# Value products and modulation chunks issued in a row, the chunks spread between the steps of the q projection, five weight pieces loaded ahead

## The chip, the cores and the metric

The kernel runs on one core of a Trainium2 chip. Its time is the device time of one execution in microseconds. The matrix engine is called PE here (PEld is its weight load, which overlaps with it), the vector engine DVE, the scalar engine ACT, the general-purpose engine POOL, and the engine that issues most of the loads SP.

## What is computed

One inference step of a two-layer trunk on 512 latent tokens and 128 context tokens of width 1024, in 32-bit floats. Layer 0 is gated attention with 16 query heads and 4 key-value heads of width 64; layer 1 is a gated linear recurrence. In both layers the input is first modulated:

```python
mod = jax.nn.silu(cond) @ w + b            # shift, scale and gate, 3 x 1024, for two conditions
h   = x * (1.0 + scale) + shift
q, k, v, g = split(h @ w_in)               # attention: q 1024, k 256, v 256, g 1024 columns
q, k = rms_norm(q) , rms_norm(k)           # and axial rotary positions on the latent tokens
s = einsum('qd,sd->qs', q, keys) / 8       # 128 cached keys and 512 own ones for latent tokens
o = einsum('qs,sd->qd', softmax(s), vals)
out = (o * silu(g)) @ w_out
x = layer_norm(alpha * x + gate * out)
```

The modulation of layer 1 (shift, scale, gate) and the gate of layer 0 are not needed in the attention; they are computed beside it.

## The kernel before, in words

The work runs in five stages: a lead-in (modulation of layer 0, keys and values), the gates' and the first q projection, the attention, the output projection of layer 0 with its normalisation, and layer 1 with its own output projection. A tile scheduler takes the program's operations in their written order, reorders them by priority and by its own estimate of what is ready, and writes one in-order queue for each engine. Within a queue an instruction that waits holds up all behind it.

**Attention.** The work is cut into 36 units: for each of the 4 key-value heads c one unit for the context tokens and 8 for the latent ones (a query head and a half of the tokens). A unit has two `front` steps (scores into a PSUM tile `sc`, row maximum `nm` on DVE, exponential into `p` on ACT, later a division on POOL), and three transposing steps `trans`, each of which transposes blocks of `p` on PE into a PSUM tile `pt` and copies them to SBUF tiles `pts`: two copies of 128x512 on ACT and a last one of 128x256 on DVE (L728). When two units of a pair are done, `apply` multiplies the values by both of them: five key blocks k, each with two products of 64 output rows (`av_mms`, L750). The product of j=0 fills PSUM partitions 0 to 63 and that of j=1 partitions 64 to 127, so the two use different columns of the PE array. A unit's time is spent on all four engines, and the units are interleaved by `att_gen`.

**Side work.** While the attention runs, `weave` gives a list of side jobs a fraction `SIDE_B` of a step for each step of the attention. In order they are: the projection of the next head's q (`q_gen`: two weight pieces, 15 token tiles of 24 products over the three heads that are made here, a chain of RMS norm and rotation over ACT, DVE and POOL, and a transposition `qps`), then some modulation chunks (`ada_gen`), and so on for three heads; after them the last modulation chunks, which wait until the attention has reached its last head, then the first pieces of the output weights and a split of the gated output. When a head's first unit is due and its q is not finished, `side.until` runs the side work without pause until it is.

**A modulation chunk** needs two weight pieces of 512 KB. `ada_part` (L262) multiplies one piece with the conditions: four products, each into 32 of the 128 output partitions, so that they use four different column groups of the array. Two such parts are summed in PSUM; then come a copy to SBUF (L276), four small products with a selector (L285) and an addition. There are 16 chunks, handed out to four places by `ADA_CUT`.

**Loads.** `pump` issues the pieces in a fixed order on SP while fewer than `RAW_AHEAD` wait to be used. The pieces lie in the pool `rawp`.

## Time and profile before

| | us |
|---|---|
| three runs, median | 894.47 |
| three runs, lowest and highest | 894.38, 896.09 |
| the profiled execution | 891.1 |
| its span, first to last instruction | 889.3 |
| PE busy in it | 844.8 |
| attention stage, about 135 to 370 us: PE busy | 225.56 of 235.00 |
| layer 1 until its last head, 450 to 790 us: PE busy | 339.67 of 340.00 |
| last stretch, 790 to 889.3 us: PE busy | 81.62 of 99.30 |

The profile is a trace of one execution. In a row of the timeline stand the start in us, the duration in us, the engine, the line of the kernel, the operation, what it writes and reads, and how many instructions were merged; a product of two 32-bit tiles (L750, L262, L285, L305) shows as two PE instructions. A value in brackets is the idle time ahead of the row and what ended it. The end of a PE instruction is modelled and overlaps the next one's start, so the time that a piece of work takes on PE is read from start to start.

### The profile page before, as it was taken

The numbers are of one execution on the slowest core, as the hardware profiler recorded it, in microseconds if no ns is written. First come the engines' busy times: TensorE is split into PE (matmuls) and PEld (weight loads), VectorE is DVE, ScalarE is ACT, GpSimd is POOL, SyncE is SP. The second block draws the span as 40 slices with busy tenths as digits, with TensorE's granted clock in tenths as the row PEclk, the third lists the DMA queues.
The fourth block names the chain that finished last, engine by engine and source line by source line (L and its number), as shares of the span: only waits on it lengthen the run. The fifth ranks groups of instructions, "written<-read, shape, count | busy, mean of one in ns | idle before, by whom it ended". The sixth has DMA issues, their size and how long they took to land.

```text
span 889.3 us, 19146 instructions
## 1 busy us (share of the span) xinstructions
PE 844.8 (95%) x8076; PEld 736.4 (83%) x8076; DVE 539.0 (61%) x960; ACT 371.2 (42%) x732; POOL 212.6 (24%) x247
## 2 busy tenths in 40 slices
PE   6898999989999899999999999999999999988995
PEld 3588999858858656778899999999999999986774
DVE  3466335646655644676446677576768585758495
ACT  2232437545554745522244454444444444443200
POOL 0032003323323724510000133233333224110110
PEclk9999999999999999999999999999999999998998
DMA  9831210042051066271131313232332313232121
GB/s 359 328 107 54 81 39 25 2 164 75 1 194 45 3 218 208 90 242 48 57 117 51 102 56 117 63 98 77 91 95 79 101 55 107 64 111 99 54 95 71
DMA packets 30182, 89.84 MB, mean 101 GB/s; under 512 B 4401, under 2 KB 9009, under 8 KB 29073
## 3 DMA queue, kind: packets, MB, share of 16 engines
q1 hardware_dynamic: 19728, 72.03, 24.1%
q0 software_dynamic: 3168, 9.31, 3.7%
q10 hardware_dynamic: 7200, 7.29, 2.6%
q8 instruction: 63, 1.03, 0.5%
q14 instruction: 23, 0.18, 0.1%
HBM read 79.44 MB, written 9.18 MB: 100 GB/s over the span
## 4 chain that ended last, share of the span: by engine, by line
PE 76%; DMA 8%; DVE 7%; POOL 3%; ACT 3%; issue 2%; ACTq 0%; DVEq 0%; POOLq 0%
PE rps L1106 7%; PE rps L1107 6%; PE rps L1108 6%; PE vgps L1096 5%; PE pot L750 4%; PE vgps L1098 4%; PE vgps L1097 4%; PE pt L832 4%; DMA raw<-in_ada_w 3%; PE outp L984 3%; PE outp L985 3%; PE outp L986 3%; PE lv L1236 2%; PE adaps L262 2%; PE sc L723 2%
## 5 line engine op out<-in xcount | busy, mean ns | idle before, releaser
L1106 PE MATMUL rps<-h1hi,rhi 128*128 128x320 f32 x368 | 118.2, 321 | 0.0
L1107 PE MATMUL rps<-h1lo,rhi 128*128 128x320 f32 x368 | 113.7, 309 | 0.0
L1108 PE MATMUL rps<-h1hi,rlo 128*128 128x320 f32 x368 | 113.3, 308 | 0.0
L825 POOL TENSOR_SCALAR p<-p,rc 128x640 f32<-128x640 f32 x64 | 52.1, 816 | 104.1 <-DVE rc L824 101.2
L1106 PEld LDWEIGHTS rps<-h1hi,rhi 128*128 128x128 f32 x368 | 69.1, 188 | 1.3
L1107 PEld LDWEIGHTS rps<-h1lo,rhi 128*128 128x128 f32 x368 | 69.3, 188 | 0.0
L1108 PEld LDWEIGHTS rps<-h1hi,rlo 128*128 128x128 f32 x368 | 69.1, 188 | 0.0
L820 ACT ACTIVATE p<-sc,nm 128x640 f32<-128x640 f32 x64 | 51.1, 798 | 41.3 <-DVE nm L817 33.4
L817 DVE TENSOR_REDUCE nm<-sc 128x1 f32<-128x640 f32 x64 | 52.4, 820 | 24.3 <-PE sc L724 23.6
L222 DVE TENSOR_TENSOR rlo<-raw,rhi 128x1024 fp32r<-128x1024 f32 x32 | 46.1, 1441 | 33.9 <-ACT rhi L221 33.9
L1264 POOL COPY At<-near 32x160 f32<-32x160 f32 x32 | 14.0, 437 | 196.6 <-DVE near L1226 195.6
L1214 ACT COPY kc<-A 128x640 f32<-128x640 f32 x40 | 32.2, 805 | 59.0 <-DVE A L1245 51.6
L221 ACT CAST rhi<-raw 128x1024 fp32r<-128x1024 f32 x32 | 33.6, 1049 | 51.6 <-PE rps L1107 47.4
L832 PE MATMUL pt<-ident,p 128*128 128x128 f32 x320 | 51.2, 279 | 1.4 <-DVE pts L728 0.8
L1096 PE MATMUL vgps<-rhi,h1hi 128*128 128x256 f32 x180 | 51.4, 286 | 1.2 <-ACT h1hi L938 1.2
L1098 PE MATMUL vgps<-rhi,h1lo 128*128 128x256 f32 x180 | 50.5, 280 | 0.4 <-DVE h1lo L939 0.4
L1097 PE MATMUL vgps<-rlo,h1hi 128*128 128x256 f32 x180 | 50.5, 280 | 0.0
L750 PE MATMUL pot<-pts,vv 128*64 128x256 f32 x320 | 50.0, 390 | 0.0
L832 PEld LDWEIGHTS pt<-ident,p 128*128 128x128 f32 x320 | 36.8, 142 | 12.9 <-issue 6.7
L728 ACT COPY pts<-pt 128x512 f32<-128x512 f32 x64 | 36.0, 588 | 23.5 <-PE pt L832 23.2
L723 PE MATMUL sc<-kk,X 128*128 128x320 f32 x128 | 43.2, 345 | 0.4 <-ACT p L820 0.4
L332 PE MATMUL gps<-hhi,whi 128*128 128x320 f32 x128 | 40.8, 319 | 2.4 <-ACT X L582 2.4
(257 smaller groups left out, 2399.2 us busy)
## 6 DMA issues: line engine op xcount, KB each, us to landing
raw<-in_rec_w_in SPq DMA_DIRECT2D x40, 512.0 KB, 3.8
raw<-in_ada_w SPq DMA_DIRECT2D x32, 512.0 KB, 4.4
raw<-in_ada_w SPq DMA_DIRECT2D x8, 1024.0 KB, 11.3
raw<-in_attn_w_in SPq DMA_DIRECT2D x16, 512.0 KB, 4.2
raw<-in_attn_w_out SPq DMA_DIRECT2D x8, 512.0 KB, 4.4
raw<-in_rec_w_out SPq DMA_DIRECT2D x8, 512.0 KB, 4.1
h<-in_xT SPq DMA_DIRECT2D x8, 320.0 KB, 10.8
x1d<-y SPq DMA_DIRECT2D x5, 512.0 KB, 2.6
```

What stands on the lines that cost most here:

```text
L723: nc.tensor.matmul(out, X[:, h, t0:t0 + P], kk[:, c, k0:k1], start=True, stop=False)
L750: nc.tensor.matmul(pot[j * HD:(j + 1) * HD, :CW], vv[:, slot, c * HD:(c + 1) * HD], moving[j], start=first, stop=last)
L817: nc.vector.tensor_reduce(nm[:, 0:1], sc[:, :, :320], AX.XY, ALU.max, negate=True)
L820: nc.scalar.activation(halves(p[:]), sc[:, :, :320], AF.Exp, bias=nm[:, 0:1], accum_out=su[:, 0:1])
L825: nc.gpsimd.tensor_scalar(p, p, rs[:, 0:1], 1.0, ALU.mult, ALU.mult)
L832: nc.tensor.transpose(pt[:, i * 256 + q * P:i * 256 + (q + 1) * P], ps[q][:, (k0 + i) * P:(k0 + i + 1) * P], ident)
L1096: nc.tensor.matmul(out, h1hi[:, k, t], hi, start=(k == 0), stop=False)
L1097: nc.tensor.matmul(out, h1hi[:, k, t], lo, start=False, stop=False)
L1098: nc.tensor.matmul(out, h1lo[:, k, t], hi, start=False, stop=(k == KT - 1))
L1106: nc.tensor.matmul(ps[:, j, :320], hi[:, k, :], h1hi[:, k, t], start=(k == 0), stop=False)
L1107: nc.tensor.matmul(ps[:, j, :320], hi[:, k, :], h1lo[:, k, t], start=False, stop=False)
L1108: nc.tensor.matmul(ps[:, j, :320], lo[:, k, :], h1hi[:, k, t], start=False, stop=(k == KT - 1))
```

## The change

The lines of the changed kernel lie 1 to 13 lines further down: L262 becomes L263, L285 becomes L286, L580 becomes L582, L723 and L724 become L725 and L726, L750 becomes L752, L832 becomes L834.

- `apply` is written under a raised priority and takes the key blocks in the order 4, 0, 1, 2, 3, and in each block j=1 ahead of j=0.
- `ada_gen` takes both pieces of a chunk at once and issues all eight products, the second piece's ahead of the first's.
- `mixed` lays modulation chunks between the steps of the q projection: for each q step it owes 0.36 of a chunk step. The chunks are handed out 3, 3, 3 and 7 instead of 4, 4, 4 and 4, and the share of side work is 0.85 instead of 0.7.
- Five pieces are loaded ahead instead of two, in six buffers of 4 KB per partition instead of three. The room that POOL's transfers use for their descriptors is set to 4096 bytes.

```diff
-ADA_CUT = (4, 8, 12)
+ADA_CUT = (3, 6, 9)
...
-RAW_AHEAD = 2
+RAW_AHEAD = 5
...
-SIDE_B = 0.7
+SIDE_B = 0.85
+MIX = 0.36
...
-    rawp = ctx.enter_context(pool("rawp", 3))
+    rawp = ctx.enter_context(pool("rawp", 6))
...
-    def ada_part(ps, i, raw):
+    def ada_part(ps, i, raw, first=0):
         for q in range(4):
             nc.tensor.matmul(ps[32 * q:32 * q + 32, :CW], sil[:, 4 * i + q, :], raw[:, q * CW:(q + 1) * CW],
-                             start=(i == 0), stop=(i == 1))
+                             start=(i == first), stop=(i != first))
         pump()
...
             ps = bank1("adaps")
-            ada_mms(ps, l, c, 0)
+            both = [take((f"ada_w{l}", c, i)) for i in range(2)]
+            for i in (1, 0):
+                ada_part(ps, i, both[i], 1)
+            yield
             if last:
                 last()
             last = todo and ada_out(*todo)
-            yield
-            ada_mms(ps, l, c, 1)
             yield
             todo = (l, c, ada_row(ps))
...
-        for j in range(2):
+        for j in (1, 0):
             nc.tensor.matmul(pot[j * HD:(j + 1) * HD, :CW], vv[:, slot, c * HD:(c + 1) * HD], moving[j], start=first, stop=last)
...
-                for k in range(5):
-                    av_mms(pot, k, c, [mine[0, k], mine[1, k]], k == 0, k == 4)
+                with tc.high_priority():
+                    for k in (4, 0, 1, 2, 3):
+                        av_mms(pot, k, c, [mine[0, k], mine[1, k]], k == 4, k == 3)
...
+    def mixed(q, ada):
+        owed = 0.0
+        for _ in q:
+            yield
+            owed += MIX
+            while owed >= 1.0:
+                owed -= 1.0
+                if next(ada, True) is None:
+                    yield
+        yield from ada
+
     for c in range(1, 4):
-        side.items.append((f"q{c}", q_next(c), lambda c=c: front_of[0] >= c - 1))
-        side.items.append(("a", ada_gen(ADA_B[c - 1])))
+        side.items.append((f"q{c}", mixed(q_next(c), ada_gen(ADA_B[c - 1])), lambda c=c: front_of[0] >= c - 1))
...
-    nc = _bacc.Bacc("TRN2", target_bir_lowering=False, num_devices=1)
+    nc = _bacc.Bacc("TRN2", target_bir_lowering=False, num_devices=1, dynamic_dma_scratch_size=4096)
```

How the queues move is shown at three places of PE's queue. First, the fourth value product (`pot`), in the attention of the first head, before:

```order
L262 MATMUL adaps<-raw,sil 32x256 x4
L750 MATMUL pot<-pts,vv 64x256
L832 MATMUL pt<-ident,p 128x128 x2
L794 MATMUL ptp<-ident,pp 128x128 x4
L750 MATMUL pot<-pts,vv 64x256 x2
L305 MATMUL gateps<-ident,gcol 128x128 x4
L285 MATMUL adaps_2108<-small,row 128x2 x2
L750 MATMUL pot<-pts,vv 64x256 x7
L305 MATMUL gateps<-ident,gcol 128x128 x4
```

The same product of the changed kernel:

```order
L834 MATMUL pt<-ident,p 128x128 x2
L725 MATMUL sc<-kk,X_1377 128x320
L726 MATMUL sc<-klo,X_1377 128x320
L796 MATMUL ptp<-ident,pp 128x128 x4
L263 MATMUL adaps<-raw,sil 32x256
L752 MATMUL pot<-pts,vv 64x256 x10
L263 MATMUL adaps<-raw,sil 32x256 x7
```

Its ten products stood in three pieces of 1, 2 and 7 and now stand in one; here it cuts a modulation chunk in two. Over the whole queue the 16 value products of the latent units stood in 43 pieces and now stand in 16, the 4 of the context units in 5 and now in 4.

Second, modulation chunks (`adaps`) in the side work of the first head, before, right behind the last transposition of a projected q (`qps`):

```order
L580 MATMUL qps<-identr,qs_1900 128x128 x4
L262 MATMUL adaps<-raw,sil 32x256 x4
L832 MATMUL pt<-ident,p 128x128 x4
L262 MATMUL adaps<-raw,sil 32x256 x4
L832 MATMUL pt<-ident,p 128x128 x4
L262 MATMUL adaps<-raw,sil 32x256 x4
```

A chunk of the changed kernel, in the midst of the q projection (`qmm`):

```order
L343 MATMUL qmm<-whi,hlo 128x256
L834 MATMUL pt<-ident,p 128x128 x4
L263 MATMUL adaps<-raw,sil 32x256 x8
L834 MATMUL pt<-ident,p 128x128 x4
L725 MATMUL sc<-kk,X_511 128x320
L726 MATMUL sc<-klo,X_511 128x320
```

The two halves of a chunk stand together; from the attention's start on, the 16 chunks stood in 32 pieces and now stand in 18.

Third, what stands between a unit's last two transpositions (`pt` x2) and the end of its value product, before:

```order
L832 MATMUL pt<-ident,p 128x128 x2
L724 MATMUL sc<-klo,X_505 128x320
L723 MATMUL sc<-kk,X_505 128x320
L724 MATMUL sc<-klo,X_505 128x320
L750 MATMUL pot<-pts,vv 64x256 x9
L580 MATMUL qps<-identr,qs_1900 128x128 x4
```

and in the changed kernel, one product earlier:

```order
L834 MATMUL pt<-ident,p 128x128 x2
L725 MATMUL sc<-kk,X_511 128x320
L726 MATMUL sc<-klo,X_511 128x320
L725 MATMUL sc<-kk,X_511 128x320
L726 MATMUL sc<-klo,X_511 128x320
L582 MATMUL qps<-identr,qs_1609 128x128 x3
L752 MATMUL pot<-pts,vv 64x256 x10
```

Before, the block of nine began with a product of an earlier key block, and the product that needs the last transpositions came at its end; now the first of the ten needs them.

## The prediction

> **What bounds the kernel now.** The first view is the busy time of each engine by stage (columns: stretch; length, PE, PEld, DVE, ACT, POOL busy with instruction counts, granted clock, DMA share, GB/s).
>
> ```profile
> 135.00:370.00 235.00, 225.56 (x1762) 172.08 (x1761) 133.24 (x297) 130.88 (x284) 83.77 (x86) 1.00 0.27 89
> 450.00:790.00 340.00, 339.67 (x4408) 328.97 (x4407) 225.24 (x347) 152.67 (x291) 89.06 (x122) 1.00 0.29 86
> 790.00:889.30 99.30, 81.62 (x683) 66.23 (x682) 66.24 (x113) 19.57 (x46) 12.34 (x16) 0.93 0.24 84
> ```
>
> PE is the bound nearly everywhere. The change touches the attention (first row), where no other engine is busy for more than 133 of 235 us, and the loads of every stage. From 450 to 790 us PE stands still for 0.33 us in all, so loads that come earlier have nothing to give there.
>
> The groups of the attention by shape show what the value products cost:
>
> ```profile
> L750 PE MATMUL pot<-pts,vv 128*64 128x256 f32 x320 | 50.0, 390 | 0.0
> ```
>
> One instruction takes 390 ns, yet 320 of them fill only 50.0 us: products in different columns of the array overlap. So PE busy hides a loss: its sum grows when such work is cut up. The timeline shows the size. Uncut, then a block cut in three (PE rows, start and duration; two instructions are one product):
>
> ```profile
> 158.27 2.38 PE L750 MATMUL pot<-pts,vv 128*64 128x256 f32 x20
> 160.58 0.38 PE L339 MATMUL qmm<-whi,hhi 128*128 128x256 f32 x1
> ...
> 199.43 0.65 PE L750 MATMUL pot<-pts,vv 128*64 128x256 f32 x2
> 200.00 0.44 PE L832 MATMUL pt<-ident,p 128*128 128x128 f32 x2
> 200.28 0.60 PE L794 MATMUL ptp<-ident,pp 128*128 128x128 f32 x4
> 200.81 0.65 PE L750 MATMUL pot<-pts,vv 128*64 128x256 f32 x4
> 201.39 1.16 PE L305 MATMUL gateps<-ident,gcol 128*128 128x128 f32 x8
> ...
> 202.82 1.94 PE L750 MATMUL pot<-pts,vv 128*64 128x256 f32 x14
> 204.69 0.49 PE L305 MATMUL gateps<-ident,gcol 128*128 128x128 f32 x2
> ```
>
> From start to start, ten products in a row take 160.58 - 158.27 = 2.31 us. In pieces they take 0.57 (one product) + 0.58 (two) + 1.87 (seven) = 3.02 us. One product costs as much as two, since its partner's columns stay empty. A piece of p pairs, an odd one counted up, follows 0.15 + 0.43 p: 0.58 for one, 1.87 for four, 2.30 for five. The row ahead also hands over later: the four `ptp` take 0.53 us up to the piece, where 0.11 us each would be 0.44. So a piece costs 0.24 us beside its pairs.
>
> **Value products in a row.** In the old queue the 16 blocks stand in 43 pieces with 94 pairs, counted up: 43 x 0.24 + 94 x 0.43 = 50.7 us, which the 50.0 us of the group bear out. In the new queue they stand in 16 pieces with 80 pairs: 16 x 0.24 + 80 x 0.43 = 38.2 us. That is -12.5 us. The context units' two products go from 5 pieces to 4: -0.7 us.
>
> **Chunks in a row.** A half chunk is four products in four column groups, and two halves may stand together (this one did by chance):
>
> ```profile
> 187.56 0.64 PE L262 MATMUL adaps<-raw,sil 128*32 128x256 f32 x8
> 188.13 0.61 PE L285 MATMUL adaps<-small,row 128*128 128x2 f32 x4
> ...
> 249.96 1.07 PE L262 MATMUL adaps<-raw,sil 128*32 128x256 f32 x16
> 250.96 0.33 PE L723 MATMUL pscp<-kk,X 128*128 128x128 f32 x1
> ```
>
> Alone a half takes 0.57 us and a whole chunk 1.00 us, each with 0.09 us of later handing over. Before: 31 halves apart and one together, 31 x 0.66 + 1.09 = 21.6 us. After: 14 whole ones and two cut by a value product into 1 and 7 products (0.66 + 1.09 each), 14 x 1.09 + 2 x 1.75 = 18.8 us. That is -2.8 us. PE's own work thus falls by 12.5 + 0.7 + 2.8 = 16.0 us; every other PE instruction of the stage is still there.
>
> **Five pieces ahead.** With three buffers a chunk's second piece is often not there:
>
> ```profile
> 188.26 0.33 SPq L210 DMA_DIRECT2D raw<-in_ada_w  x1
> 192.42 0.64 PE L262 MATMUL adaps<-raw,sil 128*32 128x256 f32 x8 [1.07 <-DVE rcp L785]
> 316.41 0.64 PE L262 MATMUL adaps<-raw,sil 128*32 128x256 f32 x8 [0.97 <-DVE nm L817]
> ...
> PE adaps L262 <- DMA raw<-in_ada_w: 0.6, 2, 0.3
> ...
> raw<-in_ada_w SPq DMA_DIRECT2D x32, 512.0 KB, 4.4
> ...
> GB/s 359 328 107 54 81 39 25 2 164 75 1 194 45 3 218 208 90 242 48 57 117 51 102 56 117 63 98 77 91 95 79 101 55 107 64 111 99 54 95 71
> ```
>
> The wait at 192.42 is named for DVE, but a load issued at 188.26 with a usual 4.4 us to land ends just there. I read both named for DVE as loads; with the two that are named for a load (0.6) that is 1.07 + 0.97 + 0.6 = 2.6 us, gone with five ahead: -2.6 us. The last seven chunks come in a burst, 2.2 to 2.8 us of PE work apart, and bring 14 pieces. Six lie ready; eight more at 359 GB/s take 8 x 1.46 = 11.7 us, and the seventh chunk stands some 17 us behind the first. So the burst is covered, by about a landing's 4.4 us.
>
> **The new wait.** The first product of a block now needs the last transposition's copy on DVE, and behind it on PE wait all later scores, with DVE's maxima and ACT's exponentials behind those. How late is that copy?
>
> ```profile
> 151.03 0.38 PE L832 MATMUL pt<-ident,p 128*128 128x128 f32 x2
> 151.54 0.31 PE L723 MATMUL sc<-kk,X 128*128 128x320 f32 x1
> 151.69 0.31 PE L724 MATMUL sc<-klo,X 128*128 128x320 f32 x1
> ...
> 151.45 0.42 DVE L728 COPY pts<-pt 128x256 f32<-128x256 f32 x1 [1.16 <-PE pt L832]
> ...
> 162.70 0.38 PE L832 MATMUL pt<-ident,p 128*128 128x128 f32 x2
> 162.90 0.82 DVE L817 TENSOR_REDUCE nm<-sc 128x1 f32<-128x640 f32 x1 [2.60 <-PE sc L724]
> 163.97 0.41 DVE L728 COPY pts<-pt 128x256 f32<-128x256 f32 x1
> ...
> 365.11 0.42 DVE L728 COPY pts<-pt 128x256 f32<-128x256 f32 x1 [0.50 <-PE pt L832]
> ...
> 184.81 0.51 PE L580 MATMUL qps<-identr,qs 128*128 128x128 f32 x4 [1.17 <-DVE qs L573]
> 185.25 0.63 PE L262 MATMUL adaps<-raw,sil 128*32 128x256 f32 x6
> ```
>
> The second of such a pair starts 0.11 us after the first. From there to the copy's end it is 0.73 us where DVE is free (151.14 to 151.87) and 1.58 us behind a maximum and an output (162.81 to 164.38). Over the 32 copies, the first at 151.45 and the last at 365.11, the mean is 1.10, the worst 3.43, and 19 lie at 0.73 to 0.80. The cover is the PE work that the new queue puts between: 0.11 + 4 scores x 0.147 (0.15 from start to start above) + 3 `qps` x 0.081 (four take 0.44 ahead of a piece, 0.09 of it the handing over) = 0.94 us for the block shown in the third place above. Worked out so, the 16 covers are 1.50, 0.94, 0.40, 1.80, 0.86, 0.99, 0.62, 1.31, 1.18, 1.31, 0.77, 0.70, 1.37, 0.51, 0.91 and 0.11 us; before, the product that needed the copy mostly had 2 to 7 us. If every copy took 0.73, PE would wait 0.33 + 0.11 + 0.03 + 0.22 + 0.62 = 1.3 us in all; at 1.58 it would be 10.2. The 32 measured delays against each cover give 5.4 on average. I take +5.4, bounds 1.3 and 10.2.
>
> **The end of each q projection** is still forced, since `until` is still there:
>
> ```profile
> PE qps L580 <- DVE qs L573: 4.2, 3, 1.7
> ```
>
> Three waits, 4.2 us. PE work between the last `qmm` and the last `qps`, by the queues with the same durations: 6.8, 5.3, 6.6 us before, 5.4, 6.5, 6.6 after. One end loses 1.4 us of cover, one gains 1.2: nothing in sum, give or take 1.5.
>
> **Shared banks.** Three single PSUM banks serve `qmm`, `pt`, `qps` and the chunks. Nine chunks now run while a bank is held by a half-made q. The chunks' copies to SBUF and PE's transpositions then turn in the remaining two. No row shows this case; the bounds are nothing (the scheduler places around it) and nine times a copy of that size (0.42 in the rows above), about 4 us; nearer to nothing, as the scheduler orders by what is free, so I take +1.0.
>
> **The tail.** At the last head ACT's casts of the output weights wait for a load, and the recurrence's copies queue behind:
>
> ```profile
> 805.97 1.04 ACT L221 CAST w<-raw 128x1024 fp32r<-128x1024 f32 x1 [2.90 <-DMA raw<-in_rec_w_out]
> 807.93 0.83 DVE L1250 TENSOR_TENSOR A<-A,T 128x640 f32<-128x640 f32 x1 [2.29 <-ACT kc L1214]
> 808.90 0.55 PE L1236 MATMUL lv<-A,kc 128*32 128x32 f32 x40 [0.97 <-DVE A L1250]
> ...
> 800.00:810.00 10.00, 6.85 (x98) 5.49 (x99) 7.71 (x11) 5.95 (x8) 0.00 (x0) 0.66 0.67 233
> 802.18 0.76 PE L1236 MATMUL lv<-A,kc 128*32 128x32 f32 x40 [3.45 <-ACT kc L1214]
> ```
>
> ACT's 2.90 becomes 0.97 of PE wait; after that PE is busy to 840 us. With the pieces there I take -1.0, bounds 0 (DVE's splits of the pieces now run closer together ahead of A) and -2.9 (all of ACT's wait). The longer wait at 802.18 does not hang on a load and stays. [...]
>
> **Sum.** -16.0 - 2.6 + 5.4 + 1.0 - 1.0 = -13.2 us. The profiled execution goes from 891.1 to 877.9 (span 889.3 to 876.1); the median of the runs lies 3.4 above the profiled one, 894.47 to 881.3 us.
>
> **The rivals.**
> (a) Copies are rarely late, because in the new order DVE has little ahead of them: wait 1.3, banks 0. -16.0 - 2.6 + 1.3 - 1.0 = -18.3, 876 us. For it: 19 of 32 delays are at the minimum. Against it: the covers are short.
> (b) Late copies each time and held banks: -16.0 - 2.6 + 10.2 + 4 - 0 = -4.4, 890 us. For it: thirteen of 32 delays are over 0.8, and a faster PE leaves DVE and ACT less time per unit.
> (c) Slower: the bank held by q becomes the bound. About 100 transposing groups share what is left. If each waited as long as one DVE copy less its overlap, 0.25 us, +25 on -13.2 gives 906 us; the point of balance is 0.13 us a group. For it: three banks for four users. Against it: before, q held a bank as well while the transpositions ran.
> (d) The softmax chain is the real bound, so that PE's saving turns into idle time; only the loads' wait is won, -2.6, 892 us. Against it: DVE and ACT are busy 57% of the stage.
> (e) POOL's smaller descriptor room makes its transfers wait for each other. It loads and stores five quarter tiles (`rx`) four times over in layer 1:
>
> ```profile
> rx<-x1d POOLq DMA_DIRECT2D x20, 128.0 KB, 3.7
> ```
>
> 40 transfers at 3.7 us would hold POOL for 148 of 340 us, where it now works 89; they would fit, unless they fall ahead of its part in the recurrence. At 2 us for each of 8 heads, +16 on -13.2 gives 897 us. No row shows the room's use. [...]
>
> **How the numbers follow.** Forecast 0.50 (881, own range 878 to 886), (a) 0.18, (b) 0.17, (d) 0.05, (c) 0.07, (e) 0.03. 0.2% is 1.8 us, about what a measurement of this kernel tells from no change. Faster: the forecast, (a), (b) and half of (d), 0.88. Same: 0.04. Slower: 0.08. The range, from (a) with a better tail to (b): 873.5 to 890.
>
> **What would show it.** Right: `pot` in 16 rows of x20, its group at 34 to 40 us instead of 50.0, attention some 12 us shorter, no row of L262 waiting for `raw`, waits of PE on DVE `pts` at some `pot` rows. Wrong, if `pot` still takes 50 us, if PE's new idle time at `pot`, `pt` or `adaps` exceeds 10 us, or if layer 1 is no longer full.

## The result and the profile after

The changed kernel takes 883.80 us (median of 4 runs, 883.61 to 885.16), the kernel before in the same series 895.03 us (894.38 to 896.09): ratio 0.9879, 95% interval 0.9864 to 0.9893, 11.2 us faster. The forecast was 881.3 us. The sum came nearly right; two of its largest terms did not, as the experiments show.

The profiled execution of the changed kernel took 885.16 us, the longest of its four runs, span 883.4. By stage (columns as in the prediction): the attention, from the first `pscp` to the first `outp`; the output projection, from there to the first `vgps`; layer 1, from the first `lv` to the last `rps`:

```profile
134.14:362.24 228.10, 213.36 (x1759) 172.50 (x1757) 131.44 (x297) 130.24 (x282) 86.68 (x85) 0.99 0.27 91
362.24:423.10 60.86, 60.44 (x273) 48.50 (x274) 45.78 (x75) 20.07 (x33) 13.84 (x8) 1.00 0.40 147
469.23:791.75 322.52, 320.47 (x4269) 309.69 (x4268) 216.07 (x336) 143.55 (x288) 86.84 (x124) 1.00 0.29 82
```

and the kernel before over the same stages:

```profile
134.45:367.98 233.53, 224.09 (x1759) 170.96 (x1757) 133.24 (x297) 129.21 (x282) 82.53 (x85) 1.00 0.27 89
367.98:429.63 61.65, 60.67 (x273) 48.39 (x274) 44.00 (x75) 20.37 (x33) 11.90 (x8) 1.00 0.43 145
475.77:796.27 320.50, 320.17 (x4269) 309.61 (x4268) 214.97 (x336) 144.12 (x288) 90.39 (x124) 1.00 0.29 83
```

The attention is only 5.4 us shorter, though PE is busy 10.7 us less: PE's idle time grew from 9.4 to 14.7 us. The granted clock of 0.99 is two stretches of 3.41 us at 0.5, from 192.03 and from 301.26 us, which cost the stage 3.4 us; the kernel before has none there. Layer 1, which was to stay as it was, is 2.0 us longer. The groups of the changed kernel's attention by line (busy us, mean ns, idle before and its releasers) show where the idle time went:

```profile
L834 PE MATMUL pt<-ident,p 128*128 128x128 f32 x320 | 52.1, 285 | 5.4 <-POOL p L827 3.2 <-DVE qn L524 0.9 <-ACT X L584 0.8
L725 PE MATMUL sc<-kk,X 128*128 128x320 f32 x128 | 44.1, 352 | 2.4 <-ACT p L822 2.1
L752 PE MATMUL pot<-pts,vv 128*64 128x256 f32 x320 | 38.1, 384 | 1.0 <-DVE pts L730 1.0
L263 PE MATMUL adaps<-raw,sil 128*32 128x256 f32 x256 | 18.4, 385 | 0.7 <-ACT pts L730 0.7
L582 PE MATMUL qps<-identr,qs 128*128 128x128 f32 x60 | 8.3, 254 | 4.7 <-DVE qs L575 3.0 <-DVE rc L826 1.1 <-ACT pts L730 0.5
```

`pot` fell from 50.0 to 38.1 us and no chunk waits for a load, as forecast. But PE waits little for the copy behind `pot` (1.0 us), and much for the softmax chain: ACT's exponentials (`p`, L822) hold the scores back, GpSimd's scaling (`p`, L827) the transpositions.

Because busy times of overlapping groups don't add, the text below uses another account, worked out from all PE rows of the attention: each row's time to the start of the next one, less the idle time, put down to the row's tile; the idle time is put down to the row that waited. It adds up to the stage (us, work + idle). The work contains what stretches at half clock cost: 3.4 us in the changed kernel, 1.7 in `e_ld`, some 8 in `e_av`, nothing in the other four.

```
          before       five ahead   + chunks     + products    only         klast        mix30
                       (e_ld)       (e_noav)     (after)       products(e_av)
pot       47.3+0.0     45.1+0.0     46.8+0.0     37.0+1.0      39.8+2.9     39.9+1.4     37.0+1.0
sc        45.8+0.4     44.9+0.0     44.4+0.0     46.9+2.4      48.1+1.8     46.7+2.6     45.0+3.2
pt        37.2+1.4     38.2+1.3     37.4+2.8     38.4+5.4      38.1+5.7     35.7+2.3     37.6+4.7
qmm       45.5+0.0     45.4+0.0     45.1+0.0     46.2+0.0      44.8+0.0     46.5+0.0     46.0+0.8
adaps     26.0+2.9     27.5+0.4     22.9+0.0     23.5+0.7      28.6+4.5     25.1+0.7     23.9+0.0
qps        5.6+4.2      5.7+4.2      5.6+3.3      6.4+4.7       6.1+1.6      6.0+1.5      6.4+0.4
all      224.1+9.4    222.9+6.5    218.8+6.6    213.4+14.7    221.6+17.1   215.0+9.0    210.9+12.0
stage      233.5        229.4        225.4        228.1         238.7        224.0        222.9
```

### The profile page after: what moved, and what is told of

Read it like the earlier page. It is cut to its first block, busy times and chain, and to the rows that moved or that the text cites. A ratio compares the mean times of both kernels' runs of the same rounds, so it can differ in the third digit from the quotient of the medians.

```text
span 883.4 us, 19132 instructions
## 1 busy us (share of the span) xinstructions
PE 833.2 (94%) x8076; PEld 737.2 (83%) x8076; DVE 540.5 (61%) x960; ACT 371.3 (42%) x732; POOL 214.7 (24%) x247
## 4 chain that ended last, share of the span: by engine, by line
PE 81%; DVE 6%; DMA 4%; ACT 3%; issue 2%; POOL 2%; DVEq 0%; ACTq 0%; SPq 0%; POOLq 0%
PE rps L1119 6%; PE rps L1120 6%; PE rps L1121 6%; PE vgps L1109 5%; PE vgps L1111 4%; PE vgps L1110 4%; PE outp L997 4%; PE outp L999 4%; PE outp L998 4%; PE pot L752 4%; PE pt L834 3%; PE lv L1249 2%; PE adaps L263 2%; PE sc L725 2%; PE gps L334 2%
## 5 line engine op out<-in xcount | busy, mean ns | idle before, releaser
L827 POOL TENSOR_SCALAR p<-p,rc 128x640 f32<-128x640 f32 x64 | 54.3, 850 | 96.1 <-DVE rc L826 84.2
L223 DVE TENSOR_TENSOR rlo<-raw,rhi 128x1024 fp32r<-128x1024 f32 x32 | 48.3, 1510 | 34.9 <-ACT rhi L222 34.9
L822 ACT ACTIVATE p<-sc,nm 128x640 f32<-128x640 f32 x64 | 51.1, 800 | 25.7 <-DVE nm L819 18.5
L1277 POOL COPY At<-near 32x160 f32<-32x160 f32 x32 | 11.1, 347 | 192.9 <-DVE near L1239 191.9
L222 ACT CAST rhi<-raw 128x1024 fp32r<-128x1024 f32 x32 | 33.6, 1050 | 56.9 <-PE rps L1120 52.8
L834 PE MATMUL pt<-ident,p 128*128 128x128 f32 x320 | 52.1, 285 | 5.4 <-POOL p L827 3.2
L834 PEld LDWEIGHTS pt<-ident,p 128*128 128x128 f32 x320 | 38.7, 146 | 13.3 <-POOL p L827 4.6
L725 PE MATMUL sc<-kk,X 128*128 128x320 f32 x128 | 44.1, 352 | 2.4 <-ACT p L822 2.1
L1109 PE MATMUL vgps<-wspare,h1hi 128*128 128x256 f32 x140 | 41.5, 297 | 0.0
## 6 DMA issues: line engine op xcount, KB each, us to landing
raw<-in_ada_w SPq DMA_DIRECT2D x8, 1024.0 KB, 11.2
```

Of the source, the lines that this page charges most:

```text
L725: nc.tensor.matmul(out, X[:, h, t0:t0 + P], kk[:, c, k0:k1], start=True, stop=False)
L822: nc.scalar.activation(halves(p[:]), sc[:, :, :320], AF.Exp, bias=nm[:, 0:1], accum_out=su[:, 0:1])
L827: nc.gpsimd.tensor_scalar(p, p, rs[:, 0:1], 1.0, ALU.mult, ALU.mult)
L834: nc.tensor.transpose(pt[:, i * 256 + q * P:i * 256 + (q + 1) * P], ps[q][:, (k0 + i) * P:(k0 + i + 1) * P], ident)
L1109: nc.tensor.matmul(out, h1hi[:, k, t], hi, start=(k == 0), stop=False)
```

## Which part brought the gain

The first four kernels take the change apart. Each is timed against the kernel before (894.59 us, 17 runs).

**Only the value products in a row.**

```diff
-        for j in range(2):
+        for j in (1, 0):
...
-                for k in range(5):
-                    av_mms(pot, k, c, [mine[0, k], mine[1, k]], k == 0, k == 4)
+                with tc.high_priority():
+                    for k in (4, 0, 1, 2, 3):
+                        av_mms(pot, k, c, [mine[0, k], mine[1, k]], k == 4, k == 3)
```

> The kernel before with only the value products in a row (last transposed group first, two column halves swapped); chunks and loads as before. Its queue holds the 16 blocks in 17 pieces with 80 pairs: 17 x 0.24 + 80 x 0.43 = 38.5 us for the pot group instead of 50.0. Theory (the forecast's terms): -12 us of PE work less +5.4 us of new waits, so 6 to 9 us faster, ratio 0.990 to 0.993; the stretch of layer 1 from its first lv to its last rps stays at 314.2 us. Rival (the saving turns into idle time, the whole gain is from loads and chunks): within 2 us of before, ratio 0.998 to 1.002.

Measured: 895.06 us (12 runs, 890.01 to 901.43), ratio 1.0001, interval 0.9974 to 1.0027. The theory fell, the rival held. In its profile (an execution of 898.46 us) the work on `pot` fell by 7.5 us, but the idle time rose from 9.4 to 17.1 us; groups of its attention:

```profile
L832 PE MATMUL pt<-ident,p 128*128 128x128 f32 x320 | 52.5, 286 | 5.7 <-POOL p L825 3.4 <-DVE qn L522 1.7 <-DVE pts L728 0.3
L750 PE MATMUL pot<-pts,vv 128*64 128x256 f32 x320 | 40.7, 402 | 2.9 <-DVE pts L728 2.8
L262 PE MATMUL adaps<-raw,sil 128*32 128x256 f32 x256 | 23.5, 418 | 4.5 <-DMA raw<-in_ada_w 4.5
```

The granted clock of the stage was 0.96, where the kernel before had 1.00: four stretches at 0.5 lost 8.5 us of the stage (each stretch's length times one less its clock).

**The change without the value products in a row** (the same lines put back).

> The changed kernel with the value products put back as before (not in a row), chunks in a row and five pieces ahead kept. Theory (the forecast's terms): -2.8 chunks, -2.6 loads, +1.0 banks, -1.0 tail, and +2.0 in layer 1 as the profile after shows it: -3.4 us, ratio about 0.996; the pot group stays at about 50 us. Rival (the value products bring nothing on the path): as fast as the whole change, ratio 0.988.

Measured: 883.32 us (6 runs, 881.62 to 884.76), ratio 0.9877, interval 0.9852 to 0.9901. This is as fast as the whole change: the rival held. So the value products in a row brought nothing, alone or with the rest, that these intervals (some 2.3 us either way) can tell from zero. The three largest of PE's waits in this kernel's attention (line, releaser, us in total, times, longest):

```profile
PE qps L582 <- DVE qs L575: 2.6, 3, 1.4
PE pt L834 <- DVE shsc L294: 1.9, 1, 1.9
PE pt L834 <- POOL p L827: 0.8, 2, 0.4
```

No score waits for an exponential here, and GpSimd's scaling is late by 0.8 us, not 3.2. The 1.9 us are a wait for a PSUM bank: the transposition reads nothing of `shsc`, but with `shsc` DVE empties the bank of a chunk.

**Only five pieces ahead.**

```diff
-RAW_AHEAD = 2
+RAW_AHEAD = 5
-    rawp = ctx.enter_context(pool("rawp", 3))
+    rawp = ctx.enter_context(pool("rawp", 6))
-    nc = _bacc.Bacc("TRN2", target_bir_lowering=False, num_devices=1)
+    nc = _bacc.Bacc("TRN2", target_bir_lowering=False, num_devices=1, dynamic_dma_scratch_size=4096)
```

> The kernel before with only five weight pieces ahead in six buffers and the smaller descriptor room. The forecast: -2.6 for the attention's loads and -1.0 in the tail, ratio 0.996, layer 1 untouched at 314.2 us from its first lv to its last rps. Theory after seeing the profile of the change: the early pieces let DVE split weights ahead of the recurrence, its fourth pass over A takes 1.36 instead of 0.93 us in most heads, and PE waits 0.34 us a head: layer 1 takes 316.2 us, which leaves -1.6 us, ratio 0.998.

Measured: 886.15 us (6 runs, 885.65 to 889.15), ratio 0.9916, interval 0.9890 to 0.9941: 8.4 us faster, more than twice the forecast. Layer 1 from its first `lv` to its last `rps` takes 322.5 us in all kernels with six buffers and 320.5 in the kernel before (the 314.2 and 316.2 in the expectations are of a window that ends some 6.3 us before the last `rps`; the difference is the same). So the loads alone are the larger part of the gain. From this kernel to `e_noav`, which adds the chunks in a row, their spreading between the q steps and the new shares of side work, it is another 886.15 - 883.32 = 2.8 us, by medians taken side by side; no run takes these three apart.

**Two pieces ahead for layer 1's weights alone**, five elsewhere:

```diff
-            if len(ahead) >= (RAW_START if start else RAW_AHEAD):
+            if len(ahead) >= (RAW_START if start else 2 if order[0][0] == "rec_w_in" else RAW_AHEAD):
```

> The changed kernel, but the weights of layer 1's input (rec_w_in) are loaded only two pieces ahead again; all other pieces five ahead. Theory (early loads disturb layer 1): the stretch from the first lv to the last rps returns to 314.2 us, 2.0 us less than in the changed kernel, ratio about 0.9857. Rival (the 2.0 us are a rhythm that the heads fall into from how the stage starts, whatever the loads do): 316.2 us and ratio 0.988 as in the changed kernel.

Measured: 884.44 us (6 runs), ratio 0.9889, interval 0.9865 to 0.9912, layer 1 still 322.5 us. The theory in that form fell; what sets layer 1 is taken up below.

## Why the loads brought more than the profile of before showed

**The kernel before, profiled once more.**

> The kernel before, unchanged, profiled again beside the others: its profiled execution of 891.1 us lies 3.5 us under its median, and five pieces ahead alone brought 8.4 us where its rows showed 2.6 us of load waits. Theory (the waits for loads differ from execution to execution and are larger in most): an execution over 893 us shows more than 2.6 us of PE waiting for weight loads in the attention and granted clocks of 0.5 behind them. Rival (the difference lies in another stage): the attention takes 233.5 us again, and the lead-in, layer 1 or the tail is longer.

Measured: 893.37 us, span 891.4. The attention took 235.2 us, and its waits for weights were larger than in the first profile:

```profile
PE qps L580 <- DVE qs L573: 4.2, 3, 1.7
PE adaps L262 <- DMA raw<-in_ada_w: 3.6, 5, 1.2
PE adaps L262 <- DVE nm L817: 1.0, 1, 1.0
```

With the wait named for `nm`, which by the prediction's reading is a load, that is 4.6 us instead of 2.6. The stages of this execution against those of `e_ld` (span 884.6) give the 6.8 us between them: attention 235.23 to 229.38 (-5.85), of it 4.2 us of the chunks' waits and 2.2 us of work on `pot`, as with earlier loads the scheduler cuts the value products into 34 pieces instead of 43; output projection 62.61 to 60.90 (-1.71); layer 1 +1.94; what follows its last `rps` 92.29 to 91.08 (-1.21). By their times (893.37 and 886.38) the two are 7.0 us apart; the remaining 1.4 us to the 8.4 lie in where they stand to the medians that the 8.4 compare (1.2 under, 0.2 over). The rival is partly right too: the output projection gains. There ACT's casts of its weights waited for loads in the kernel before, in this second profile of it

```profile
ACT wohi L221 <- DMA raw<-in_attn_w_out: 8.9, 3, 4.8
```

and the profile after has no such row in that stage. The first profile of the kernel before has it too, with 7.9 us in three waits; how much of it reaches PE was not taken apart. The kernel before ran from 890.5 to 900.1 us over the three series of runs (43 runs), each kernel with five ahead within 4 us (4 to 6 runs). That short looking ahead makes the time uncertain as well as longer is not shown by it: the next kernel has it too, and its 11 runs lie within 2.6 us.

**The change with short looking ahead** (two pieces in three buffers; the smaller descriptor room stays).

> The changed kernel with two pieces ahead in three buffers again; the smaller descriptor room stays. Theory (a whole chunk needs both its pieces at once, so short looking ahead costs more here than in the kernel before): the waits of the chunks' products for weight loads exceed the 4.6 us of the kernel before, the clock falls behind some of them, and the time is 890 to 898 us, ratio 0.996 to 1.004. Layer 1: DVE's queue has the early weight split two operations later again, so 320.5 us from its first lv to its last rps; rival for that stage (the smaller descriptor room slows it): 322.5 us. Rival for the whole (loads hardly matter once work is in a row): 884 us, ratio 0.988.

Measured: 892.81 us (11 runs, 891.22 to 893.75) against 892.44, ratio 1.0003, interval 0.9993 to 1.0014. Without the early loads nothing is left of the change, and the smaller descriptor room, which is still there, brings nothing that can be seen. The chunks' products now need both pieces at once; the waits in its attention, and then windows of its last quarter (granted clock in the last column but two):

```profile
PE adaps L263 <- DMA raw<-in_ada_w: 6.6, 4, 5.6
```

```profile
342.00:345.00 3.00, 0.16 (x2) 0.07 (x1) 0.27 (x2) 0.00 (x0) 0.00 (x0) 0.79 0.65 172
345.00:350.00 5.00, 2.27 (x18) 1.08 (x19) 0.28 (x1) 0.00 (x0) 0.00 (x0) 0.50 0.39 126
350.00:356.00 6.00, 6.00 (x29) 5.33 (x29) 1.59 (x8) 4.71 (x8) 3.70 (x3) 0.50 0.48 165
```

One wait of 5.6 us, to 347.73 us, is followed by more than 6 us at half clock. The stage has 20.8 us of idle time, and the clock cost it 8.5 us by the lengths of its stretches at 0.5, 2.0 of them while PE stood still. Layer 1 is back at 320.6 us, with the smaller descriptor room still there: that room is not what lengthens layer 1.

## Why the value products in a row brought nothing

From the kernel without them (`e_noav`) to the changed one, PE's work falls by 5.4 us and its idle time rises by 8.1 us. Without the 3.4 us at half clock the work falls by 8.8, so that work and waits balance even then (the two profiles are the longest of four runs and the shortest of six, so their difference is larger than that of the medians). In the last quarter of the attention, from the first `pscp` of the last head on, where no q projection runs beside, the changed kernel is even slower, 52.8 against 50.4 us at full clock in both; first it, then the kernel without the row:

```profile
309.40:362.24 52.84, 47.44 (x416) 33.65 (x414) 27.21 (x68) 30.47 (x68) 20.17 (x22) 1.00 0.47 160
```

```profile
308.80:359.23 50.43, 49.91 (x413) 34.25 (x413) 26.23 (x66) 28.08 (x64) 19.21 (x21) 1.00 0.48 168
```

No engine behind the scores is busy for more than 31 of 53 us, which speaks for the chain's delay, not its rate. The PE rows say how. In the changed kernel (idle time in brackets):

```profile
350.17 0.88 PE L834 MATMUL pt<-ident,p 128*128 128x128 f32 x6 [0.39 <-POOL p L827]
...
351.47 0.38 PE L834 MATMUL pt<-ident,p 128*128 128x128 f32 x2
352.95 0.33 PE L834 MATMUL pt<-ident,p 128*128 128x128 f32 x1 [1.10 <-POOL p L827]
...
353.91 2.38 PE L752 MATMUL pot<-pts,vv 128*64 128x256 f32 x20
```

and in the kernel without the row:

```profile
349.87 0.38 PE L834 MATMUL pt<-ident,p 128*128 128x128 f32 x2
350.18 0.65 PE L752 MATMUL pot<-pts,vv 128*64 128x256 f32 x4
350.76 0.33 PE L834 MATMUL pt<-ident,p 128*128 128x128 f32 x1
...
351.73 0.65 PE L752 MATMUL pot<-pts,vv 128*64 128x256 f32 x4
352.31 0.88 PE L834 MATMUL pt<-ident,p 128*128 128x128 f32 x6
```

There pieces of a product or two stand between the transpositions, while maximum, exponential and scaling of the next scores run. In a row, all ten stand behind the last transposition and PE waits.

**Old order of the key tiles.**

```diff
-                    for k in (4, 0, 1, 2, 3):
-                        av_mms(pot, k, c, [mine[0, k], mine[1, k]], k == 4, k == 3)
+                    for k in range(5):
+                        av_mms(pot, k, c, [mine[0, k], mine[1, k]], k == 0, k == 4)
```

> The changed kernel with the five key tiles in their old order (the group that is transposed last comes last), the two column halves still swapped and still ahead of other ready work. Its queue holds the 16 blocks in 35 pieces of whole pairs, 80 pairs: 35 x 0.24 + 80 x 0.43 = 42.8 us, against 45 pieces and 92 pairs (50.4 us) without the change to the products, and 16 and 80 (38.2 us) with it. Theory (the pieces were filler between the scores and the transpositions, and one row of 2.3 us takes that filler away): PE's idle time in the attention stays near the 6.6 us of the kernel without the row, and the pairs' 7 us are won: 4 to 7 us faster than the changed kernel, ratio 0.980 to 0.984. Rival (the chain through DVE, ACT and POOL sets the pace and PE's work is hidden under it anyway): no faster than the changed kernel, ratio 0.988.

Measured: 881.34 us (6 runs, 880.71 to 883.11) against 894.76, ratio 0.9843, interval 0.9814 to 0.9871. Against the changed kernel's 883.80 that is 2.5 us, less than the theory's 4 to 7, though of the right sign. (Differences to the changed kernel are here and below between medians of different series of runs; by the ratios, 0.9843 against 0.9879, the intervals overlap.) In the account above `pot` comes back to 39.9 us of work (2.9 more than in a row), and the idle time falls from 14.7 to 9.0 us. Against the kernel without the row the theory's 7 us of `pot` are won (46.8 to 39.9), but `sc` and `adaps` take 4.5 us more there. The scores' wait for exponentials stays (2.6 us); that for the scaling and for the q projections' ends falls.

**The row in three groups of four.**

```diff
-                with tc.high_priority():
-                    for k in (4, 0, 1, 2, 3):
-                        av_mms(pot, k, c, [mine[0, k], mine[1, k]], k == 4, k == 3)
+                ks = (4, 0, 1, 2, 3) if c < 3 else range(5)
+                with ExitStack() as st:
+                    if c < 3:
+                        st.enter_context(tc.high_priority())
+                    for k in ks:
+                        av_mms(pot, k, c, [mine[0, k], mine[1, k]], k == ks[0], k == ks[-1])
```

> The changed kernel, but in the last of the four key/value groups, where no q projection runs beside, the value products stand as they did before (old order, no raised priority; the halves still swapped). Theory (lost filler): the last quarter of the attention falls from 52.8 us back to some 50.5 us, 2.3 us faster than the changed kernel, ratio 0.985. Rival (the row costs the same everywhere and nothing in the last quarter alone): within 1 us of it, ratio 0.988.

Measured: 881.90 us (6 runs, 880.34 to 882.60), ratio 0.9844, interval 0.9816 to 0.9872: 1.9 us under the changed kernel. The last quarter takes 50.8 us, as the theory of lost filler says; the first three (each from a head's first `pscp` to the next head's) differ from the changed kernel's by 1.5, 0.0 and 0.1 us, the first through one stretch at half clock that this execution does not have (shown below).

**More cover for the ends of the q projection.**

```diff
-MIX = 0.36
+MIX = 0.30
```

> The changed kernel with MIX 0.30 for 0.36, so that fewer chunks come between the steps of the q projection and its ends get more PE work as cover (by the queue 7.4, 7.7 and 7.2 us to the last transpositions instead of 4.8, 5.5 and 5.5). Theory (the 2.76 us wait at the end of the second projection and the granted clock of 0.5 behind it, 1.7 us, go away): some 4 us faster than the changed kernel, ratio 0.9835. Rival (DVE's two weight splits, not the cover, hold that projection's end, and the waits move along): ratio 0.988.

Measured: 880.35 us (6 runs, 878.75 to 881.93), ratio 0.9832, interval 0.9800 to 0.9863, 3.4 us under the changed kernel; the forecast was some 4. The idle time at `qps` falls from 4.7 to 0.4 us. What the one long wait in the changed kernel had cost, its PE rows and its windows show:

```profile
188.39 0.46 PE L582 MATMUL qps<-identr,qs 128*128 128x128 f32 x4
191.61 0.52 PE L582 MATMUL qps<-identr,qs 128*128 128x128 f32 x4 [2.76 <-DVE qs L575]
```

```profile
190.00:192.00 2.00, 0.39 (x5) 0.42 (x6) 1.06 (x4) 1.01 (x3) 0.92 (x1) 1.00 0.32 125
192.00:195.00 3.00, 3.00 (x17) 3.00 (x16) 0.00 (x0) 1.76 (x3) 0.13 (x1) 0.51 0.00 0
195.00:198.00 3.00, 3.00 (x33) 2.34 (x33) 1.07 (x3) 0.28 (x1) 0.00 (x0) 0.93 0.00 0
```

Half clock for 3.4 us takes 1.7 us more beside the 2.76. It need not come: in the kernel with the row in three groups the same wait (2.77 us, to 192.45 us) was not followed by it:

```profile
193.00:196.00 3.00, 3.00 (x28) 2.99 (x26) 0.00 (x0) 1.56 (x3) 0.00 (x0) 1.00 0.00 0
```
With `MIX` 0.30 the clock was 1.00 throughout the stage in the profiled execution, the fastest of its six.

In these profiles lost cover is not what made the wait. Between the last `qmm` and that `qps` PE has 7.2 us of work; at the same place the kernel before has 7.3 and waits 1.17 us. What is longer is the way through DVE, whose queue holds this ahead of the norm `qn`:

```profile
184.40 1.21 DVE L223 TENSOR_TENSOR wlo<-raw,whi 128x1024 fp32r<-128x1024 f32 x1
...
185.59 1.75 DVE L223 TENSOR_TENSOR wlo<-raw,whi 128x1024 fp32r<-128x1024 f32 x1
188.29 0.69 DVE L307 COPY gate<-gateps 128x512 f32<-128x512 f32 x1 [0.95 <-PE gateps L306]
...
189.63 0.41 DVE L524 TENSOR_TENSOR qn<-qmm,rstd 128x256 f32<-128x256 f32 x1
```

Two splits of the next weights stand there, and a copy that waits for `gateps`, which PE starts at 187.09 us, behind a value product in a row (184.78 to 187.09). In the kernel before no split stands between. So the rival is right about the splits, but the wait did not move along: with `MIX` 0.30 PE has 10.8 us of work there, which covers it.

**Both, in two ways.** First `MIX` 0.30 with the old order of the key tiles:

> The changed kernel with both edits at once: MIX 0.30 and the five key tiles in their old order (pieces of whole pairs). Alone they brought 3.4 and 2.5 us against the changed kernel. Theory (two separate losses: the end of the q projection with the clock behind it, and the filler between scores and transpositions): the gains add to 5 to 6 us, 878 us, ratio 0.981 to 0.982. Rival (both remove the same idle time): as the better one alone, 880.3 us, ratio 0.983.

Measured: 882.57 us (4 runs, 881.49 to 883.58) against 892.44, ratio 0.9896, interval 0.9883 to 0.9910. Not even the rival's 880.3: the two edits don't add. The idle time at `qps` was already 1.5 us with the old order, and is 2.3 here; the stage takes 224.6 us, against 224.0 and 222.9 with the one and the other. Its profiled lead-in, which no edit touches, lost 3.4 us to the clock.

Then `MIX` 0.30 with the row in three groups of four:

> The changed kernel with MIX 0.30, and in the last key/value group the value products as before (old order, no raised priority). Alone they brought 3.4 and 1.9 us. Theory (separate losses): 878.5 us, ratio 0.982, and the last quarter of the attention at 50.8 us, the second and third at 54 to 55 us. Rival (the same idle time): 880.3 us, ratio 0.983.

Measured: 877.97 us (4 runs, 877.50 to 881.10), ratio 0.9852, interval 0.9835 to 0.9870. By the times the gains add, by the ratios (0.9852 against 0.9832) they don't. In the profile they do: the last quarter takes 51.1 us, the second and third 54.0 and 54.6, the whole stage 222.5 with 1.7 of it lost to the clock, against 222.9 with nothing lost for `MIX` alone. This is the shortest time of all kernels. Its ratio is not below that of `MIX` alone, because the kernel before was 2.3 us quicker in that series; which of the two is better is not settled.

## Layer 1

Two rows at one place of the same head show what costs layer 1 its 2 us. DVE's second pass over A at the level of 32, and the GpSimd rows beside it, before:

```profile
682.51 0.93 DVE L1250 TENSOR_TENSOR A<-A,Tb 128x640 f32<-128x640 f32 x1
...
680.89 1.87 POOL L1264 COPY At<-near 32x160 f32<-32x160 f32 x4 [16.31 <-DVE near L1226]
682.85 1.18 POOL L1347 TENSOR_TENSOR rx<-rx,ln_g 128x256 f32<-128x256 f32 x1
```

and after:

```profile
676.41 0.82 DVE L1258 TENSOR_TENSOR A<-A,Tb 128x640 f32<-128x640 f32 x1 [1.57 <-PE lv L1255]
677.15 1.36 DVE L1263 TENSOR_TENSOR A<-A,Tb 128x640 f32<-128x640 f32 x1
678.66 0.80 PE L1255 MATMUL lv<-A 128*64 128x64 f32 x20 [0.34 <-DVE A L1263]
...
676.44 1.39 POOL L1360 TENSOR_TENSOR rx<-rx,ln_g 128x256 f32<-128x256 f32 x1
677.91 1.19 POOL L1361 TENSOR_TENSOR rx<-rx,ln_b 128x256 f32<-128x256 f32 x1
```

With the buffers free, the weight split `wspare` stands five operations earlier in DVE's order, three of them passes over A. The passes shift against GpSimd's work, and one of them now begins while `rx` runs: 1.36 us instead of 0.93 (0.82 where GpSimd is idle), and PE waits 0.34 us. That happens in six heads, in the kernel before in one. It is the order, not the depth: with two pieces ahead in six buffers `wspare` keeps the early place and layer 1 its 322.5 us, with three buffers the late place returns and 320.6 us with it. In these rows it matters which begins first: the pass at 676.41 begins 0.03 us ahead of `rx` and takes its 0.82 us, while `rx` takes 1.39 us, where two such steps from 508.13 us, with no pass over A beside them, take 0.73 each; the pass at 677.15 begins with 0.68 us of `rx` still to run and takes 1.36 us, 0.54 us longer. In the kernel before, `rx` begins 0.34 us behind the pass of 0.93.

**GpSimd's step moved ahead**, on the kernel with `MIX` 0.30 and the old order of key tiles:

```diff
+            if lev == 3:
+                residual.step()
             if lev == 4:
...
-                residual.step()
```

> The kernel with MIX 0.30 and the old order of key tiles, and in layer 1 GpSimd's step on the residual (rx) is issued at the third doubling of the recurrence instead of behind its copies to At at the fourth. Theory (layer 1's 2.0 us come from DVE's pass over A running beside GpSimd's rx, 1.36 us instead of 0.82 to 0.93, with PE waiting 0.34 us a head for it): that pass takes under 0.95 us, and layer 1 from its first lv to its last rps takes 320.5 instead of 322.5 us, 2 us less than the same kernel without this edit. Rival (the weight split ahead of A shifts the chain, GpSimd has no part in it): 322.5 us and no difference.

Measured: 881.09 us (5 runs), ratio 0.9879, interval 0.9863 to 0.9894, against 0.9896 without the edit; the intervals overlap. Layer 1 takes 322.0 us. The pass still meets `rx` in three heads (1.25 us) and waits remain, 1.3 us in all:

```profile
PE lv L1249 <- DVE A L1263: 1.3, 4, 0.6
```

So the move did not part the two, and gives neither theory its test by the time; that PE's wait goes with the overlap is seen only row by row.

## Why the prediction came near, and where it was wrong

- **What bounds the kernel.** PE is the bound by busy time, but in the changed kernel's attention it stands still for 14.7 us, mostly behind DVE, ACT and GpSimd, of which none is busy for more than 131 of 228 us. The prediction read 133 of 235 us as room. Room in rate is not room in delay. The attention, some 12 us shorter by its signs, is 5.4 shorter.
- **Value products in a row, -12.5.** The work was mis-sized a little: 47.3 to 37.0 us is -10.3, so that a piece costs about 0.16 us beside its pairs, (10.3 - 14 x 0.43) / 27, not 0.24: the handing over did not go away with the pieces. The context units' -0.7 came (`potp` and `ptp` together 4.97 to 4.12).
- **The new wait, +5.4.** This is the step that failed. It is about as large as the growth of the idle time (+5.3), but it isn't that wait: PE waits 1.0 us for the last copy, near the lower bound of 1.3. What grew beside it stands at scores (2.1 us behind exponentials, 0.4 before) and at transpositions (3.2 behind GpSimd's scaling, 0.5 before), where the pieces had covered the softmax chain, and at shared banks (below). The prediction counted what the new order puts in front of the copy and not what it takes away from in front of everything else. With it and the clock behind it the term as a whole measures nothing: 883.80 with the row, 883.32 without.
- **Rival (d)**, that PE's saving turns into idle time, got 0.05. For the value products it was right; it was set aside because of the engines' shares. It was wrong in that the 2.8 us of the chunks' part did come through, and the loads brought more than its 2.6.
- **Rivals (a) and (e).** The premise of (a) came true, the copy is late by 1.0 us in all, and yet its 876 us did not come: like the forecast it counted no wait but that one. What POOL's transfers use of the descriptor room no run shows, and the slower transfers of (e) are not seen: with the small descriptor room and short looking ahead layer 1 takes 320.6 us.
- **Chunks in a row, -2.8, and banks, +1.0.** Together -2.8 us from `e_ld` to `e_noav`, where -1.8 was forecast; the work on `adaps` fell from 27.5 to 22.9 us there. The loss from shared banks is seen, of the forecast's kind: `e_noav` has the 1.9 us at `pt` behind `shsc`. In the changed kernel 3.3 us are named for a read that empties such a bank, where the row needs nothing else of it (`pt` behind `qn` 0.9, `X` 0.8 and `pts` 0.4, `adaps` behind `pts` 0.7, `qps` behind `pts` 0.5); in the kernel before it is 0.8 (`pt` behind `pts`).
- **Five pieces ahead, -2.6.** Mis-sized: 8.4 us with all that the early loads do, the tail included. That the two waits named for DVE were loads is borne out, as they are gone in `e_ld` (`adaps` waits 0.4 us there instead of 2.9); but the load that ends the wait at 192.42 is one issued at 187.10 and landed at 192.29, while the one shown, from 188.26, lands at 193.68. The row from which it came belongs to an execution 3.4 us under the median, and no price stood for the output projection's casts and for the products that the scheduler cuts less.
- **The end of each q projection, 0.** In sum it held: the waits for `qs` went from 4.2 to 3.0 us, all waits at `qps` from 4.2 to 4.7, within the 1.5 allowed. But one wait of 2.76 us is left instead of three of 1.2 to 1.7, at the end whose cover was to fall (6.8 to 5.4 us by the queues), and by the trace it comes from DVE's longer way (above). The 1.7 us of clock behind it had no term.
- **Layer 1, 0; the tail, -1.0.** Layer 1 lost 2.0 us through an order that the early loads changed; the prediction asked only whether loads there had waited. Its own sign of error, layer 1 no longer full, came true. From the last `rps` to the last `lv` it took 29.5 us before and 28.6 after, but 28.7 in the second profile of before: the -1.0 can't be told from that spread, though the wait of 0.97 us (1.2 in the second profile) is gone after. The wait at 802.18 stayed: 3.45 us before, 3.44 after, with the clock at 0.5 for 6.8 us there in both profiles. So no run shows the better tail that the lower end of the range, 873.5 us, counts with.

So -13.2 forecast and -11.2 measured agree by errors that cancel: the products gave 0 instead of some -8 net, the loads -8.4 instead of -3.6, the chunks with the banks -2.8 instead of -1.8. That the sum came so near is luck.

## What to carry to other kernels

Small pieces of independent work between the steps of a long dependent chain are its cover: before joining them, count for each wait what PE work will still stand in front of it, for every consumer and not only for the one whose operand moves. A saving on the busiest engine counts only as far as no new wait takes its place. And price waits for loads from more than one execution, beside the spread of the runs: the profile may be a fortunate one.

## What the hardware showed that was not expected

- Behind waits of PE of the same length the granted clock fell in one execution and not in another. After 2.76 us (changed kernel, above) it was 0.5 for 3.4 us, which takes 1.7 us more; after the same wait in the kernel with the row in three groups it stayed at 1.00. After 1.90 us (`pt`, kernel `e_noav`) it stayed at 1.00 too, but after 1.70 us (`qps`, kernel `e_ld`) it fell, and after the same 1.70 us in the kernel before it did not; `e_ld`'s windows over that wait and behind it:

```profile
306.30:308.06 1.76, 0.07 (x1) 0.02 (x1) 1.20 (x4) 0.49 (x2) 1.76 (x3) 1.00 0.00 0
308.06:311.50 3.44, 3.43 (x27) 1.82 (x28) 0.37 (x1) 1.17 (x2) 0.54 (x1) 0.68 0.33 105
```

  In the changed kernel's attention the two stretches at 0.5, from 192.03 and from 301.26 us, are 3.413 us long each and begin 109.23 us apart, 32 times that length. And no single long wait stands ahead of the second: PE waits only 0.89 and 0.58 us in the 3.4 us before it.

```profile
298.77 0.66 PE L834 MATMUL pt<-ident,p 128*128 128x128 f32 x4 [0.89 <-DVE qn L524]
...
300.30 0.44 PE L834 MATMUL pt<-ident,p 128*128 128x128 f32 x2 [0.58 <-ACT X L584]
```

- The lead-in, untouched by any edit, took 133.8 to 136.4 us over the profiled executions, with 0, 1.7 or 3.4 us of it lost to such dips: part of the spread between runs is this.
- A DVE pass of layer 1 over 640 elements takes 0.81 to 0.83 us with GpSimd idle, 0.82 where it begins 0.03 us ahead of GpSimd's `rx`, 0.93 where it begins beside the last 0.26 us of a GpSimd copy, and 1.36 where it begins with some 0.68 us of `rx` still to run. Where 0.04 to 0.06 us of `rx` are left, it takes 0.81.
